# Mixers of a trunk layer traced as many small streams in the order of an in-order model of four engines

## The chip, the cores and the metric

The kernel runs on one core of a Trainium2 chip. Its five engines are TensorE (PE in the rows; PEld is its loading of weights), VectorE (DVE), ScalarE (ACT), GpSimd (POOL) and SyncE (SP), each with an instruction stream of its own that it works off in order; semaphores tie them together, and DMA queues move data between HBM and SBUF. The metric is the device time of one execution in microseconds (us).

## The reference

One layer of a decoder trunk on a sequence of 1024 tokens and a model width of 1024, in float32: half a SwiGLU feed-forward (2816 wide), then two token mixers side by side on the normed stream, then another half feed-forward. The mixers:

```python
proj = h @ w_in[l]
(c_q, k_a, v_a, k_idx, w_idx, q_b, k_b, v_b, gate_a, gate_b) = jnp.split(proj, offsets, axis=-1)
...
# a: sparse attention
dots = jnp.einsum('bthd,bsd->bths', qi, k_idx)
score = jnp.einsum('bths,bth->bts', jax.nn.relu(dots), wi)     # lightning indexer, 8 heads of 64
_, idx = lax.top_k(score, 256)                                 # the keys that a query may see
p = softmax(q_a . gathered keys)                               # 8 heads, one shared key and value
# b: stick-breaking attention, 8 heads of 64
log_not = jnp.where(strict, jax.nn.log_sigmoid(-z), 0.0)
between = lax.cumsum(log_not, axis=3, reverse=True) - log_not
a = jnp.where(strict, jnp.exp(jax.nn.log_sigmoid(z) + between), 0.0)
o = jnp.einsum('bhts,bshd->bthd', a, v_b)
...
merged = jax.nn.sigmoid(gate_a) * (y_a @ w_o_a[l]) + jax.nn.sigmoid(gate_b) * (y_b @ w_o_b[l])
x = x + merged @ w_out[l]
```

## The kernel before

Every product of two float32 matrices is made of three TensorE products of a high and a low part (`mm3`: high by high, low by high, high by low), so each operand is split: ScalarE copies the rounded high part, VectorE (or, for weights in SBUF, GpSimd) subtracts it and leaves the low part. The two feed-forward blocks and the merge stand before and after the mixers and are not touched here.

The mixers run in three stages, told apart below by what TensorE writes to PSUM.

- **Index stage.** `latents`, `keys`, `index_queries`, `indexer` and `queries` make the rotated keys and queries of the sparse attention (`psvb`, `pska`, `pskt`, `psq`, `psqt`) and the indexer's scores (`psdot`, ScalarE's `relu`, VectorE's `u`). Beside them `fillers` multiplies h by the value weights (`psvb`) and by the weights of q_b, k_b and the gates (`psf`); the results go to HBM through a ring of three 128x512 buffers, tag `ev`: `evv` for values, `evh` and `evl` (high, low) for q and k, `evg` for gates. Each filler's weights are loaded by SP (`wqk...r`), split into `...h` on ScalarE (L226) and `...l` on GpSimd (L228). `topk` finds the 256th largest score of each query by bisection, 3 row blocks at once, counting on ScalarE (`junka`, L1005) or VectorE (`junkv`, L1014), and stores a mask `bd`.
- **Stick stage.** `sticks` makes `psz` for 8 heads and 8 row blocks; ScalarE takes both sigmoids (L1334 `left`, L1335 `sa`), VectorE a scan along the keys (L1337) and a product (L1339, `sa`). `values` turns four blocks of `sa` at a time on TensorE (`pstT`), ScalarE and VectorE split them into `pt` (L1377, L1378), and TensorE multiplies by the values into one bank `psy` (L1362, L1364). The product of key block j is traced one step behind the turn of block j+1. The rest of `fillers` runs between.
- **Sparse stage.** `logits` (`psL`), softmax on ScalarE and VectorE (`e`), `latent_values` (`pspT`, `pt`, `pso`), `head_values` (`psya`, then `yah`, `yal`), and the two output projections `psob` and `psoa` (`project`), gated on GpSimd. The first `psm` ends it.

What sets the order: the stages are Python generators. `Weave.run` resumes again and again the generator whose wants are ready earliest by a model of the engines (`COST`: a fixed time and a rate for each). Only TensorE is under `manual_schedule` (L853): its instructions stand in the order in which they were traced, and those of the other engines are ordered by the framework's scheduler. In the model those engines fill earlier gaps (`place`, L111). A generator's evacuations are traced together with the matmuls that they follow. The sparse queries (`queries`, L1292) come after all index queries (the mark `wqi`). The heads of the stick stage take turns in two sets of buffers (`qs`, `kkh`, `kkl`, L1081).

## Time and profile before

| | us |
|---|---|
| median of 3 runs (lowest, highest) | 2362.55 (2357.9, 2365.03) |
| the profiled execution's own time | 2361.66 |
| its span in the trace | 2359.9 |
| TensorE busy in the span | 2221.0 |
| VectorE busy | 1628.2 |
| ScalarE busy | 1067.6 |
| GpSimd busy | 924.7 |
| index, stick and sparse stage | 715.8 to 987.3, 1365.5 and 1576.2 |

The mean granted TensorE clock over the span is 0.978 of full speed. Of the 2.3 us between the span and the execution's own time nothing is in the trace. A group in the rows below is a line, an engine and an operation; "idle before" is time in which that engine stood still right before instructions of the group, put down to what released it last.

### The profile page before, as it was taken

Reading aid. Unit: us, or ns where it says so; the run is one execution under the profiler, and the core shown is the slowest. Engines: PE = TensorE matmul, PEld = TensorE weight load, DVE = VectorE, ACT = ScalarE, POOL = GpSimd, SP = SyncE. Lnnn points to the kernel's source line nnn. Section 1 sums busy time; section 2 is a strip of 40 time slices with the busy share of each in tenths; the row PEclk is TensorE's granted clock in tenths of the full one; section 3 lists DMA queues with packets and bytes.
Section 4 is the critical chain, followed back from the end, with each engine's and each line's share of the span. In section 5 each row is a group of like instructions: output and inputs, shape, how many; then the busy total and the mean of one; then the engine's idle time right before and its main releaser. Section 6 shows DMA issues by size and latency. Waiting matters only on the chain.

```text
span 2359.9 us, 30282 instructions
## 1 busy us (share of the span) xinstructions
PE 2221.0 (94%) x10460; PEld 1819.9 (77%) x10460; DVE 1628.2 (69%) x2598; ACT 1067.6 (45%) x2042; POOL 924.7 (39%) x673
## 2 busy tenths in 40 slices
PE   7999999999998799778888989999999999999999
PEld 6788888888888678667666778777878888888877
DVE  5766666688772778699587877773476656667675
ACT  4323323344352378766745665643333333333443
POOL 3554555332352334311222223357435555552233
PEclk9999999999999999899899999999999999999999
DMA  5232333586753444434445532537423333348755
GB/s 162 84 108 94 107 94 107 182 318 218 191 162 112 110 110 121 134 74 95 103 120 130 170 107 101 185 126 259 125 65 97 107 94 108 98 156 283 235 174 179
DMA packets 251498, 330.65 MB, mean 140 GB/s; under 512 B 19536, under 2 KB 154336, under 8 KB 251344
## 3 DMA queue, kind: packets, MB, share of 16 engines
q1 hardware_dynamic: 234224, 288.83, 40.5%
q0 software_dynamic: 7488, 24.16, 2.8%
q10 hardware_dynamic: 9632, 15.73, 1.9%
q8 instruction: 82, 1.34, 0.2%
q14 instruction: 72, 0.59, 0.1%
HBM read 234.78 MB, written 93.88 MB: 139 GB/s over the span
## 4 chain that ended last, share of the span: by engine, by line
PE 40%; DVE 12%; issue 3%; DMA 2%; ACT 2%; POOL 1%; SPq 0%; ACTq 0%; DVEq 0%; POOLq 0%
PE p L609 3%; PE p L608 3%; PE p L607 3%; DVE left L1337 3%; PE pc L398 2%; PE pc L400 2%; PE pc L399 2%; PE pa L400 2%; PE pa L399 2%; PE pd L400 2%; PE pa L398 2%; PE pd L398 2%; PE pd L399 2%; DVE sa L1339 1%; DVE junkv L1014 1%
## 5 line engine op out<-in xcount | busy, mean ns | idle before, releaser
L1005 ACT ACTIVATE junka<-u,cand 128x640 bf16<-128x640 f32 (+1 forms) x138 | 124.9, 905 | 36.8 <-DVE cand L1003 29.4
L1337 DVE TENSOR_TENSOR_SCAN left<-left 128x640 f32<-128x640 f32 (+3 forms) x64 | 94.8, 1487 | 3.5 <-ACT left L1334 3.3
L1364 PE MATMUL psy<-pt,vv 128*128 128x512 f32 (+1 forms) x96 | 37.8, 405 | 36.5 <-DVE pt L1378 29.3
L1378 DVE TENSOR_TENSOR pt<-pstT,pt 128x512 fp32r<-128x512 f32 (+1 forms) x96 | 51.0, 550 | 26.8 <-ACT pt L1377 26.8
L1390 POOL TENSOR_TENSOR yl<-yt,yh 64x512 fp32r<-64x512 f32 x16 | 26.9, 1679 | 104.7 <-ACT yh L1389 94.0
L1510 DVE TENSOR_TENSOR pt<-pspT,pt 128x512 fp32r<-128x512 f32 x72 | 48.9, 686 | 26.8 <-ACT pt L1509 26.7
L1334 ACT ACTIVATE left<-psz 128x512 f32<-128x512 f32 (+2 forms) x96 | 48.6, 506 | 35.5 <-DVE sa L1339 20.9
L1470 ACT ACTIVATE e<-e,nm 128x768 f32<-128x768 f32 (+7 forms) x64 | 49.4, 772 | 32.2 <-DVE nm L1466 31.2
L217 POOL TENSOR_TENSOR rs<-ms,mhalf 128x1 f32<-128x1 f32 (+1 forms) x41 | 35.9, 909 | 68.9 <-DVE ms L215 67.9
L1377 ACT ACTIVATE pt<-pstT 128x512 fp32r<-128x512 f32 (+1 forms) x96 | 45.2, 495 | 38.0 <-PE pstT L1373 36.4
L1461 DVE CUSTOM_DVE_ANT_0 e<-psL,bias 128x512 f32<-128x512 f32 (+3 forms) x96 | 52.0, 550 | 9.4 <-PE psL L1459 8.6
L1286 DVE SCALAR_TENSOR_TENSOR u<-relu,WI,u 128x512 f32<-128x512 f32 (+1 forms) x70 | 49.3, 723 | 12.1 <-ACT relu L1281 10.3
L1339 DVE TENSOR_TENSOR sa<-sa,left 128x639 f32<-128x639 f32 (+3 forms) x64 | 53.6, 843 | 2.7
L1364 PEld LDWEIGHTS psy<-pt,vv 128*128 128x128 f32 x96 | 19.5, 203 | 46.3 <-DVE pt L1378 37.2
L608 PE MATMUL p<-bT,bS 128*128 128x512 f32 x132 | 51.8, 393 | 2.5 <-DVE bT L309 2.5
L1509 ACT ACTIVATE pt<-pspT 128x512 fp32r<-128x512 f32 x72 | 41.4, 594 | 27.7 <-PE pspT L1504 27.3
L609 PE MATMUL p<-bT,bS 128*128 128x512 f32 x132 | 51.6, 394 | 0.8 <-POOL bS L309 0.8
L608 PE MATMUL p<-aT,aS 128*128 128x512 f32 x132 | 51.7, 392 | 0.0
L609 PE MATMUL p<-aT,aS 128*128 128x512 f32 x132 | 50.9, 393 | 0.0
L1373 PE MATMUL pstT<-ident,sa 128*128 128x128 f32 x288 | 49.1, 292 | 1.3 <-DVE sa L1339 1.3
L1335 ACT ACTIVATE sa<-psz 128x512 f32<-128x512 f32 (+2 forms) x96 | 48.8, 509 | 0.0
L1281 ACT ACTIVATE relu<-psdot 128x512 f32<-128x512 f32 (+1 forms) x80 | 39.7, 521 | 19.9 <-DVE u L1286 10.2
(3061 smaller groups left out, 8423.1 us busy)
## 6 DMA issues: line engine op xcount, KB each, us to landing
aw<-in_w_down_dram SPq DMA_DIRECT2D x33, 512.0 KB, 4.5
bw<-in_w_down_dram SPq DMA_DIRECT2D x33, 512.0 KB, 4.5
a0r<-in_w_gate_dram SPq DMA_DIRECT2D x22, 512.0 KB, 4.1
a1r<-in_w_up_dram SPq DMA_DIRECT2D x22, 512.0 KB, 4.7
b0r<-in_w_gate_dram SPq DMA_DIRECT2D x22, 512.0 KB, 3.9
b1r<-in_w_up_dram SPq DMA_DIRECT2D x22, 512.0 KB, 4.8
x<-in_x_dram SPq DMA_DIRECT2D x16, 512.0 KB, 6.0
gd<-evg ACTq DMA_DIRECT2D x32, 256.0 KB, 2.3
```

Source lines behind the costliest of these rows:

```text
L398: nc.tensor.matmul(ps, a[:, c], b[k][:, HI], start=start and k == 0, stop=False, skip_group_check=True)
L399: nc.tensor.matmul(ps, a[:, c], b[k][:, LO], start=False, stop=False, skip_group_check=True)
L400: nc.tensor.matmul(ps, a[:, l], b[k][:, HI], start=False, stop=k == 3, skip_group_check=True)
L607: nc.tensor.matmul(ps[q][m], S[:, h], T[:, HI], start=p == 0, stop=False)
L608: nc.tensor.matmul(ps[q][m], S[:, h], T[:, LO], start=False, stop=False)
L609: nc.tensor.matmul(ps[q][m], S[:, l], T[:, HI], start=False, stop=p == last)
L1005: nc.scalar.activation(junks[1][:, 0:(i + 1) * P], score[i], AF.Sign, bias=cand.bitcast(F32)[:, b:b + 1], accum_out=cnt[:, b:b + 1])
L1337: nc.vector.tensor_tensor_scan(back, back, back, 1.0, op0=ALU.mult, op1=ALU.bypass)
L1339: nc.vector.tensor_mul(a[:, 0:nk - 1], a[:, 0:nk - 1], left[:, 1:nk])
L1364: nc.tensor.matmul(yp[:, off:512], vv[:, kc], pt[:, 512 + off:1024], start=False, stop=(j == 4 * c + 3), skip_group_check=True)
L1378: nc.vector.tensor_sub(pt[:, 512 + off:1024], tp[:, off:512], f32(pt[:, off:512]))
L1461: nc.vector.tensor_tensor_reduce(e[:, c], lp[:, 0:n_], bias[:, c], 1.0, LOW, op0=ALU.add, op1=ALU.max, accum_out=mx[:, g:g + 1])
```

## The change

The instructions of the mixers stay the same in kind, and nearly in number; the feed-forwards and the merge are not changed. What changes is how their order is made, and some buffers.

- **Order.** `manual_schedule` now holds TensorE, VectorE, ScalarE and GpSimd, so all four run the instructions of the mixers in the order of tracing. Each evacuation is a stream of its own (`spawn`); it names the engine of its next step and what that needs. `run` takes the stream with the least (time at which its step can start, rank, ready time plus slack). The model's engines work strictly in order, other `COST`s are put in, and a DMA's landing is modelled (2.4 us and 0.25 MB per us). SP is not held.
- **Rings.** Every buffer ring counts who still holds a tile (`give`). The stick stage's result takes one `ev` buffer (`yh`) in place of three; `yl` and `yt` share a ring of one. The gates of the output projections have a ring of three 512-column tiles in place of one of 1024.
- **Weights.** `Feed` keeps three sets of weights under way, through all fillers and both output projections.
- **Products.** The turns of `sa` and of `e` and the products with values are separate streams, so a product can stand any number of turns behind, with the ring `pt` three deep as before.
- **Sparse queries.** `queries` starts when the indexer's keys are done (`places`), with the buffers of the odd heads as its own; heads 1 to 7 wait for its end. The second half of the latents is turned first.

The core of the diff:

```diff
+    def __call__(self, name, holds=1):
+        w = self.weave
+        w.flush()
+        old = self.live[-self.bufs] if len(self.live) >= self.bufs else None
+        assert old is None or not w.held[old.tensor.name], name
+        t = self.tiles(name, self.tag, self.bufs, self.dt, self.shape)
+        if old is not None:
+            w.base[t.tensor.name] = max(w.base[t.tensor.name], w.done[old.tensor.name] + w.HOP)
+        w.held[t.tensor.name] = holds
+        self.live = (self.live + [t])[-self.bufs:]
+        return t
...
-    COST = {"PE": (0.0, 2400.0), "DVE": (0.07, 960.0), "Activation": (0.1, 1200.0), "Pool": (0.15, 460.0)}
+    COST = {PE: (0.015, 2400.0), DVE: (0.12, 960.0), ACT: (0.1, 1250.0), POOL: (0.2, 465.0)}
...
+                if eng == SP:
+                    self.free[SP] = max(self.free[SP], t) + mb / 0.25
+                    t, eng = self.free[SP] + 3.0, "DMA"
+                else:
+                    t = max(t, self.free[eng]) + (0.55 if eng == POOL else 0.05)
+                    self.free[eng], t, eng = t, t + 2.4 + mb / 0.25, "DMA"
...
+                eng, *needs = s.need
+                ready = max(self.when(needs, eng), s.since)
+                if ready < float("inf"):
+                    rank = next((n for n in needs if isinstance(n, int)), s.rank if eng == PE else min(s.rank, 1))
+                    slack = next((n for n in needs if isinstance(n, float)), 0.0)
+                    key = max(ready, self.free[eng] if eng != SP else 0.0), rank, ready + slack
+                    if best is None or key < best[0]:
+                        best = key, s
+            assert best, [(s.gen.__name__, s.need) for s in self.streams]
+            best[1].since = best[0][0]
+            self.step(best[1])
...
-    with fp as fpool, fps as fpsum, psm as psum, tc.manual_schedule(engines={nc.tensor.engine}):
-
-
-        ended = [0.0]
+    with fp as fpool, fps as fpsum, psm as psum, tc.manual_schedule(
+            engines={nc.tensor.engine, nc.vector.engine, nc.scalar.engine, nc.gpsimd.engine}):
...
+                while self.todo and len(self.coming) < 3:
...
+        sets[4:4] = [(w_in, C_VB + 256, 256, 4 * j, 4, f"wvb1{j}") for j in range(2)]
...
+        def qk_out(ps, pr, nh_, nl_, sc, cols):
+            yield ACT, ps, (evr, 2)
+            th, tl_ = evr("evh"), evr("evl")
+            nc.scalar.activation(th, ps, AF.Copy, scale=sc)
+            put_high(qkd[nh_][pr * P:(pr + 1) * P, cols], f32(th))
+            yield DVE, ps, th
+            nc.vector.scalar_tensor_tensor(tl_, ps, sc, f32(th), op0=ALU.mult, op1=ALU.subtract)
+            give(ps, th)
+            yield POOL, tl_
+            put_low(qkd[nl_][pr * P:(pr + 1) * P, cols], f32(tl_))
+            give(tl_)
...
+                yield SP, f"qk{h // 2}", "queries" if h else None, *rings
...
+            rows = [sring(f"cqn{half}") for half in range(2)]
             for half in (1, 0):
                 nc.sync.dma_start(rows[half], cqd[half])
-            yield None
-            weave.mark("wcq")
-            for half, cqn in enumerate(rows):
+                nc.sync.dma_start(*((rope, roped), (ropeq, ropeqd))[1 - half])
+            for half in (1, 0):
+                cqn, outs = rows[half], []
                 cols = slice(half * 512, half * 512 + 512)
...
+            yield PE, "places"
+
+            spare = [here[nm][1] for nm in ("qs", "kkh", "kkl")]
+            outs = []
             for t in range(NT):
-                QS = yield from qstack(W["uq"], t, qcos, qsin, True, "qsa")
-                put_low(qad[t * P:(t + 1) * P, :], f32(QS))
-
-        weave.run([latents(), keys(), indexer(), index_queries(), queries()], more)
+                QS = yield from qstack(WQ["uq"], t, qcos, qsin, True, "qsa", spare[t % 2], qxring, spare[2])
...
+        def turned_out(tp, pt, off=0):
+            yield ACT, tp
+            nc.scalar.activation(pt[:, off:512], tp[:, off:512], AF.Copy)
+            yield DVE, tp, pt
+            nc.vector.tensor_sub(pt[:, 512 + off:1024], tp[:, off:512], f32(pt[:, off:512]))
+            give(tp)
...
+        def y_out(yp, h, c):
+            yield ACT, yp, yring
+            yl = yring("yl")
+            yt = f32(yl[0:HD])
+            nc.scalar.activation(yt, yp[HD:P, :], AF.Copy)
+            yield DVE, yp, yl
+            nc.vector.tensor_add(yt, yp[0:HD, :], yt)
+            give(yp)
+            yield ACT, yl, evr
+            yh = evr("yh")
+            nc.scalar.activation(yh[0:HD], yt, AF.Copy)
+            cols = slice(c * 512, c * 512 + 512)
+            put_high(ybd[0][h * HD:(h + 1) * HD, cols], f32(yh[0:HD]))
+            yield POOL, yl, yh
+            nc.gpsimd.tensor_tensor(yl[0:HD], yt, f32(yh[0:HD]), op=ALU.subtract)
+            put_low(ybd[1][h * HD:(h + 1) * HD, cols], yt)
+            give(yl, yh)
...
+        def value_products(h, c, pts, outs):
+            yield PE, wbank, f"vv{h}"
+            yp, vv = wbank("psy"), VV[h]
+            for j in range(4 * c + 4):
+                while len(pts) <= j:
+                    yield PE, f"pt{h}{c}{j}"
+                job, off, pt = pts[j]
+                yield PE, job, pt
+
+                kc = slice(j * P, (j + 1) * P)
+                nc.tensor.matmul(yp[:, off:512], vv[:, kc], pt[:, off:512], start=(j == 0), stop=False,
+                                 skip_group_check=True)
+                nc.tensor.matmul(yp[:, off:512], vv[:, kc], pt[:, 512 + off:1024], start=False,
+                                 stop=(j == 4 * c + 3), skip_group_check=True)
+                give(pt)
...
-                yt = f32(evr("yt"))[0:HD]
-                nc.scalar.activation(yt, yp[HD:P, :], AF.Copy)
-                nc.vector.tensor_add(yt, yp[0:HD, :], yt)
-                yh, yl = (evr(n_)[0:HD] for n_ in ("yh", "yl"))
...
+        for g, rank in ((v_loads(), 0), (values(), 0), (sticks(), 1), (head_values(), 2), (latent_values(), 3), (logits(), 4),
+                        (hidden_keys(), 1), (latent_queries(), 1), (outputs(), 6)):
```

Three places in the order of instructions.

ScalarE at the start of the mixers, before the change: `wka0h` and `wka1h` are the high parts of the latent weights, `evv` the values' high parts, `cqh` the turned query latents.

```order
L226 ACTIVATE wka0h<-wka0r 128x1056
L902 ACTIVATE evv<-psvb 128x4x64 x3
L226 ACTIVATE wka1h<-wka1r 128x1056
L1127 ACT_TABLE_LOAD
L902 ACTIVATE evv<-psvb 128x4x64
L1164 ACTIVATE KK<-pska 128x128
L1166 ACTIVATE va<-pska 128x128
L1147 ACTIVATE cqh_6025<-pscqt,gcolq 128x512
```

And after it:

```order
L972 ACTIVATE evv<-psvb 128x4x64 x5
L1257 ACTIVATE cqh_6006<-pscqt,gcolq 128x512
L1257 ACTIVATE cqh_6007<-pscqt,gcolq 128x512
L972 ACTIVATE evv<-psvb 128x4x64
L1257 ACTIVATE cqh_6006<-pscqt,gcolq 128x512
L1257 ACTIVATE cqh_6007<-pscqt,gcolq 128x512
L938 ACTIVATE wka0h<-wka0r 128x1056
L972 ACTIVATE evv<-psvb 128x4x64
```

The split of the first latent weights stood ahead of the first four `evv`; now it stands behind five or more of them and the latents, and the split of the second is further down than these rows go.

TensorE at the second turn of keys, before the change: `kdup` is the duplicated key tile that VectorE makes, `pskt` its turn, `psf` the first filler with query weights.

```order
L239 MATMUL psvb<-wvb01h,mhi_5236 128x256
L240 MATMUL psvb<-wvb01l,mhi_5236 128x256
L241 MATMUL psvb<-wvb01h,mlo_5244 128x256
L1200 MATMUL pskt<-ident,kdup 128x128 x8
L239 MATMUL psf<-mhi_5229,wqk5200h 128x512
L240 MATMUL psf<-mlo_5237,wqk5200h 128x512
L241 MATMUL psf<-mhi_5229,wqk5200l 128x512
L239 MATMUL psf<-mhi_5230,wqk5200h 128x512
L240 MATMUL psf<-mlo_5238,wqk5200h 128x512
L241 MATMUL psf<-mhi_5230,wqk5200l 128x512
L1245 MATMUL psqt<-ident,qx 128x128 x4
```

And after it:

```order
L280 MATMUL psq<-wqih,cqh_6006 128x512
L281 MATMUL psq<-wqil,cqh_6006 128x512
L282 MATMUL psq<-wqih,cql_6008 128x512
L280 MATMUL psq<-wqih,cqh_6007 128x512
L281 MATMUL psq<-wqil,cqh_6007 128x512
L282 MATMUL psq<-wqih,cql_6009 128x512
L1485 MATMUL psdot<-kih,qsi 128x512
L1486 MATMUL psdot<-kil,qsi 128x512
L1372 MATMUL pskt<-ident,kdup 128x128 x4
L1485 MATMUL psdot<-kih,qsi 128x512
L1486 MATMUL psdot<-kil,qsi 128x512
L1485 MATMUL psdot<-kih,qsi 128x512
```

The second `pskt` stood behind value products; now it stands in the middle of the indexer's first `psdot`, split in two, behind the fillers of three sets of query and key weights.

TensorE at the end of the mixers, before the change: `psya` is the product with the value up-projection, `psm` the first matmul of the merge, `psoa` the output projection of the sparse attention.

```order
L241 MATMUL psya<-oh_14161,uvl 128x256
L239 MATMUL psya<-oh_14161,uvh 128x256
L240 MATMUL psya<-ol_14162,uvh 128x256
L241 MATMUL psya<-oh_14161,uvl 128x256
L239 MATMUL psya<-oh_14161,uvh 128x256
L240 MATMUL psya<-ol_14162,uvh 128x256
L241 MATMUL psya<-oh_14161,uvl 128x256
L239 MATMUL psm<-yah_11587,woa0h 128x512
L240 MATMUL psm<-yal_11591,woa0h 128x512
```

And after it:

```order
L282 MATMUL psoa<-yah_11598,oa6l 128x512
L280 MATMUL psoa<-yah_11599,oa6h 128x512
L281 MATMUL psoa<-yal_11603,oa6h 128x512
L282 MATMUL psoa<-yah_11599,oa6l 128x512
L280 MATMUL psoa<-yah_11600,oa6h 128x512
L281 MATMUL psoa<-yal_11604,oa6h 128x512
L282 MATMUL psoa<-yah_11600,oa6l 128x512
L280 MATMUL psm<-yah_11597,woa0h 128x512
L281 MATMUL psm<-yal_11601,woa0h 128x512
```

The products of the last head values ran straight into the merge; now matmuls of `psoa` stand between.

## Rows read from the trace of the kernel before

**Rows 1.** Busy time of each engine in four stretches: the indexer (first psvb to first psz), the sticks (to the last psy), the sparse attention (to the first psm), and a stretch of the first FFN. Columns: stretch, its length, busy us and instructions of PE, PEld, DVE, ACT, POOL, mean granted TensorE clock, share and rate of the DMA engines.

```profile
715.80:987.30 271.50, 231.69 (x1292) 200.64 (x1292) 176.79 (x335) 158.57 (x330) 102.57 (x95) 0.94 0.41 117
987.30:1365.50 378.20, 323.93 (x1531) 254.49 (x1530) 316.61 (x590) 242.56 (x515) 79.07 (x53) 0.93 0.45 116
1365.50:1576.20 210.70, 199.62 (x1058) 166.60 (x1057) 157.49 (x453) 122.24 (x255) 79.80 (x69) 0.97 0.43 141
177.00:590.00 413.00, 413.00 (x1795) 336.31 (x1794) 281.68 (x351) 143.88 (x250) 179.82 (x121) 1.00 0.48 160
```

**Rows 2.** Waits of TensorE from 700 to 990 us: engine, what it was to write, its line, what it waited for; us in total, times, the longest.

```profile
PE psqt L1245 <- DVE qx L1241: 10.9, 3, 10.2
PE psdot L1278 <- ACT relu L1281: 9.2, 8, 3.4
PE pskt L1200 <- DVE kdup L1192: 9.1, 2, 8.7
PE psf L239 <- DVE evl L934: 4.9, 2, 3.4
PE psvb L239 <- DVE evv L903: 3.4, 1, 3.4
PE psvb L239 <- DVE cqn L669: 2.6, 1, 2.6
PE pska L240 <- POOL wka1l L228: 2.1, 1, 2.1
```

**Rows 3.** The same view from 990 to 1366 us.

```profile
PE psy L1364 <- DVE pt L1378: 29.3, 22, 4.4
PE psy L1362 <- ACT pt L1377: 8.1, 7, 2.4
PE psy L1364 <- DVE rem L1070: 7.0, 1, 7.0
PE psf L239 <- ACT evg L952: 5.9, 3, 5.4
```

**Rows 4.** Timeline of ScalarE from 714 us, where the latent weights are split: start, length, what; in brackets the idle time before it.

```profile
723.32 1.08 ACT L226 ACTIVATE wka0h<-wka0r 128x1056 fp32r<-128x1056 f32 x1 [9.52 <-issue]
724.31 0.64 ACT L902 ACTIVATE evv<-psvb 128x256 fp32r<-128x256 f32 x2
```

**Rows 5.** Timeline of VectorE around the second set of keys.

```profile
771.55 2.79 DVE L1182 TENSOR_TENSOR KK<-KK,rs 128x512 f32<-128x512 f32 x1
774.38 5.19 DVE L1183 TENSOR_TENSOR KK<-KK,gk 128x512 f32<-128x512 f32 x1
779.60 0.69 DVE L1187 TENSOR_TENSOR kt<-KK,rope 128x512 f32<-128x512 f32 x1
```

**Rows 6.** Timeline of GpSimd in the same stretch.

```profile
771.39 2.40 POOL L228 TENSOR_TENSOR wuql<-wuqr,wuqh 128x1024 fp32r<-128x1024 f32 x1
...
774.36 2.36 POOL L228 TENSOR_TENSOR wqk5200l<-wqk5200r,wqk5200h 128x1024 fp32r<-128x1024 f32 x1
776.66 2.35 POOL L228 TENSOR_TENSOR wqk10320l<-wqk10320r,wqk10320h 128x1024 fp32r<-128x1024 f32 x1
```

**Rows 7.** Groups of VectorE instructions in the sticks' stretch: line, what, count, busy us and mean ns of one, idle time before them and its releasers.

```profile
L1337 DVE TENSOR_TENSOR_SCAN left<-left 128x640 f32<-128x640 f32 (+3 forms) x64 | 94.8, 1487 | 3.5 <-ACT left L1334 3.3
L1339 DVE TENSOR_TENSOR sa<-sa,left 128x639 f32<-128x639 f32 (+3 forms) x64 | 53.6, 843 | 2.7
L1378 DVE TENSOR_TENSOR pt<-pstT,pt 128x512 fp32r<-128x512 f32 (+1 forms) x96 | 51.0, 550 | 26.8 <-ACT pt L1377 26.8
L1014 DVE TENSOR_SCALAR_CACHE_REDUCE junkv<-word,clow 128x1024 bf16<-128x1024 uint16 (+2 forms) x48 | 41.9, 873 | 0.7
```

**Rows 8.** Groups of GpSimd instructions in the same stretch; the sixteen splits of weights (L228) stand one by one, one of them shown.

```profile
L1390 POOL TENSOR_TENSOR yl<-yt,yh 64x512 fp32r<-64x512 f32 x15 | 25.6, 1706 | 98.3 <-ACT yh L1389 87.6 <-DMA gd<-evg 10.7
...
L228 POOL TENSOR_TENSOR wg11l<-wg11r,wg11h 128x1024 fp32r<-128x1024 f32 x1 | 2.4, 2362 | 16.5 <-ACT wg11h L226 16.5
```

**Rows 9.** DMA issues from 800 to 990 us: queue, count, KB each, median us from issue to landing.

```profile
qhd<-evh ACTq DMA_DIRECT2D x8, 256.0 KB, 5.5
qld<-evl POOLq DMA_DIRECT2D x8, 256.0 KB, 7.6
khd<-evh ACTq DMA_DIRECT2D x8, 256.0 KB, 3.1
kld<-evl POOLq DMA_DIRECT2D x8, 256.0 KB, 5.2
```

**Rows 10.** Timeline of TensorE at the end of the mixers.

```profile
1564.49 0.65 PE L1496 MATMUL pso<-pt,kkh 128*128 128x512 f32 x1 [2.89 <-ACT e L1470]
...
1567.45 0.47 PE L1504 MATMUL pspT<-ident,e 128*128 128x128 f32 x1 [0.82 <-DVE e L1473]
1568.67 0.79 PE L1496 MATMUL pso<-pt,kkh 128*128 128x512 f32 x1 [0.75 <-ACT pt L1509]
...
1576.18 0.50 PE L239 MATMUL psm<-yah,woa0h 128*128 128x512 f32 x1 [0.93 <-DVE yal L1544]
```

1033 lines of the change are left out of this document (616 added, 417 removed).

## The prediction

> **What bounds the kernel now.** I read the page's busy shares first, then busy time by stage, then TensorE's waits, then what the engines that it waits for did just before. Over the stretch of FFN in [rows 1] TensorE is busy for all of 413.0 us at full clock, 0.230 us for each of 1795 matmuls: nothing that the mixers do can shorten that. In the mixers it is busy 231.7 of 271.5, 323.9 of 378.2 and 199.6 of 210.7 us, so it stands still for 39.8, 54.3 and 11.1 us, together 105 us. Beside that the mean granted clock there is 0.94, 0.93 and 0.97. With busy time times the missing share as the price (an estimate) the lower level, 1.2 in place of 2.4 GHz, costs 13.9, 22.7 and 6.0 us. It falls after TensorE has stood still or waited in short pieces; the FFN stretch, with no gap, keeps 1.00. So some 148 us is the most that any order of the same instructions can win on TensorE, and the next limit must be looked for: in the stick stage VectorE is busy 316.6 us [rows 1], most of it scans, products and low parts [rows 7]. That stage cannot fall below some 317 us without VectorE falling too. In the other two stages VectorE has some 95 and 53 us to spare.
>
> Which wait ends last is read from [rows 2, 3]. In the index stage there are two long single ones, 10.2 us for `qx` and 8.7 us for `kdup`, and a crowd of short ones for `relu`. In the stick stage the products wait 29.3 + 8.1 us for `pt`, in 29 pieces, then once 7.0 us for `rem` and 5.9 us for gates.
>
> **The change part by part.** It neither adds nor removes work: each engine keeps nearly the same instructions. So each term is a wait that goes, stays or appears.
>
> Front of the index stage. ScalarE stood still 9.52 us with the split of `wka0h` at the head of its stream and the values' high parts behind it [rows 4]; the row names no releaser, and I take it to be the raw weights' landing. TensorE paid 3.4 us for `evv`, and 2.1 us for `wka1l` later [rows 2]. The split now stands behind the first `evv`. If the weights are late again, TensorE has values to multiply. I take 3.4 + 2.1 = 5.5 us as gone; the 2.6 us for `cqn` ends ahead of the stretch in [rows 1] and stays.
>
> Second keys. The 8.7 us for `kdup` come from VectorE: two products on 512 columns took 2.79 and 5.19 us [rows 5], where a like one took 0.69 us right after. In those 8 us GpSimd ran weight splits of 2.40, 2.36 and 2.35 us [rows 6], and the 5.19 us product ends just as the last two do. So these two products lost 6.6 us to GpSimd. The order now puts the turn behind fillers and the first `psdot`, some 38 matmuls of 0.230 us or 8.7 us more cover than before. The whole wait of 9.1 us goes, even if GpSimd holds the products as long again. Also, `qx` is behind these products on VectorE: its 10.2 us is the same jam seen from the next stream. I take 10 us of 10.9 as gone.
>
> What appears: the first query weights need buffers that come free when the value products are done, so the fillers that now give cover begin with a split on ScalarE and one of 2.36 us on GpSimd. I charge 4 us (bounds: 0, if the weights wait for nothing, and 10, the longest wait in [rows 2]).
>
> The `relu` waits (9.2 us) stay: the scores still have two such buffers. So does the 4.9 us for `evl`: queries and keys still leave through a ring of three.
>
> The clock: with the long waits gone I give back half of 13.9 us, 7 us; bounds 0 and 14.
>
> Index stage: 5.5 + 9.1 + 10 + 7 - 4 = 27.6 us less.
>
> Stick stage. The 5.9 us for `evg` has its cause in the `ev` ring: the results of a head took three of its buffers, and GpSimd waited 87.6 us for `yh` in them [rows 8]. With one buffer in place of three this goes. The 7.0 us for `rem` is a step of the mask that VectorE ran in one piece ahead of `pt`; the change yields between its steps, so it goes: 12.9 us. Of 37.4 us for `pt` I take a third, 12.5 us. Products may stand further behind turns now, but `pt` must still pass ScalarE and then VectorE, which is busy 84% of the stage, and the scans before it are the same (1487 ns on average, 64 of them, up to the next free place [rows 7]). Bounds are 0 and all 37.4. Of the clock I take a third, 8 us (0 to 23). Sum 33.4 us: the stage comes to 345 us, 28 above VectorE's busy time.
>
> Sparse stage. At its end TensorE waits 2.89, 0.82, 0.75 and 0.93 us within some 14 us and runs slowly between [rows 10]. Matmuls of `psoa` now stand behind the last attention work. They fill such gaps but came from elsewhere, where they filled others: 2 us (bounds -3 to 17, the stage's idle and clock).
>
> Sum: 27.6 + 33.4 + 2 = 63 us. The profiled execution took 2361.66, so 2298.7, say **2299 us**. That execution is 0.9 us below the median of the three runs, so I make no correction. It is 2.7% faster. What this kernel's measurement can tell from no change is about 0.3%, or 7 us.
>
> **The rule that speaks against it.** The jam in [rows 5, 6] says that a VectorE product with two inputs in SBUF stands still while GpSimd runs a product of its own.
>
> The Trainium skill, GPSIMD Engine Reference, section Key points, says the same: GpSimd shares its SBUF interfaces with VectorE, with contention against VectorE instructions in a 2-port mode or with two SBUF inputs. The trace agrees (5.19 beside 0.69 us). The model that makes the new order counts each engine alone, so by this rule its plan breaks wherever it sets a split beside a product; that is the slower rival below.
>
> **The rivals.**
>
> *Landings eat the index gain.* The new order counts on a transfer of 256 KB landing some 3.5 us after its issue; measured are 5.5 and 7.6 us for the halves of the queries, 3.1 and 5.2 us for those of the keys [rows 9]. Each of 16 halves takes two of three `ev` buffers, and they come free only upon landing. TensorE makes a half in 24 x 0.230 = 5.5 us. A landing of 7.6 us holds the next but one half by about 2 us, if no other stream fills it: 16 x 2 = 32 us. Then 2299 + 32 = 2331. For it: `psf` waited for `evl` before, and fillers now begin earlier and stand closer. Against: that wait was only 4.9 us.
>
> *Everything goes.* All idle of the index stage (39.8) and 5 us of its clock, the stick stage down to VectorE's 316.6 (61.6 less), 5 us in the sparse stage: 111 us, 2250. For it: streams are now cut small enough for any gap to be filled. Against: the plan's durations are not the chip's, and engines that work in order hand each error on.
>
> *Slower: GpSimd holds VectorE in the stick stage.* All evacuations are in order now, and nothing steps ahead of a held one. GpSimd is busy 79.1 us there [rows 1], with 15 subtractions of 1706 ns and 16 splits of 2362 ns or more [rows 8], all with two inputs. VectorE has the `sa` product, 64 times 843 ns, just in the chain scan, `sa`, turn, `pt` [rows 7]. If all 79 us came to hold that chain, TensorE would wait as much for `pt`: 2299 + 79 = 2378, slower by 0.7%. It decides from 63 us, four fifths of GpSimd's time. For it: one jam cost 6.6 us within 8. Against: before the change some of it was paid already, and scans have one input.
>
> *No change.* Each wait that goes comes back under another name, the work in front of `pt` above all, since VectorE is the busiest after TensorE: 2362 us.
>
> **How the numbers follow.** The forecast gets 0.46, landings 0.18, everything 0.12, no change 0.09, slower 0.15. Faster by over 0.3%: 0.46 + 0.18 + 0.12 = 0.76; within 0.3%: 0.09; slower: 0.15. The forecast's own range is 2275 to 2325, from half of the bounds above. The wide one takes in landings and no change, and leaves out the outer half of "everything" and the upper half of "slower": 2258 to 2366.
>
> **What would show it.** In the changed profile: no wait over 5 us for `qx` or `kdup` in the index stage, which ends some 244 us after its start; no `rem` or `evg` wait, and some 25 us for `pt`, in a stick stage of 345 us with VectorE's busy time at 305 to 320 us; a granted clock of 0.96 or more in both. Landings would show as `psf` waiting for `evl` or the DMA queues of `evh` over 20 us; contention as a mean `sa` well over 843 ns. The forecast is wrong if TensorE's idle time in the mixers falls by less than 30 or more than 80 us of its 105.

## The result and the profile after

The changed kernel takes 2347.57 us (median of 8 runs, 2343.23 to 2349.67), the kernel before 2358.61 us on the same chips (8 runs, 2353.92 to 2365.03): ratio 0.9947, 95% interval 0.9930 to 0.9964. That is faster by 0.5%, and far from the 2299 us that was forecast. Of 63 us foreseen, some 12 came (11.0 by the medians, 12.5 by the ratio).

The two profiled executions took 2361.66 and 2345.06 us, so the traces lie 5.6 us further apart than the medians. Their spans are 2359.9 and 2343.0 us, so 1.8 and 2.1 us lie outside the traces (for the kernel before it is 1.8 us and not 2.3). Busy time by stage in the changed kernel, in the columns of [rows 1]; the last row is all that follows the mixers:

```profile
715.40:974.00 258.60, 234.27 (x1299) 198.41 (x1300) 169.49 (x330) 150.89 (x311) 101.52 (x95) 0.97 0.42 120
974.00:1327.40 353.40, 308.45 (x1505) 245.20 (x1503) 325.67 (x569) 244.18 (x522) 92.80 (x54) 0.94 0.48 125
1327.40:1555.40 228.00, 203.39 (x1076) 169.20 (x1075) 159.46 (x490) 128.07 (x268) 74.37 (x67) 0.94 0.37 121
1555.40:2343.00 787.60, 775.34 (x3404) 630.38 (x3404) 487.48 (x585) 272.93 (x461) 354.37 (x232) 0.99 0.46 152
```

Against [rows 1] the index stage is 12.9 us shorter, the stick stage 24.8, and the sparse stage 17.3 us longer. What follows the mixers took 783.7 us before and takes 787.6. TensorE's idle time (length less busy time) went from 39.8, 54.3 and 11.1 us to 24.3, 45.0 and 24.6. Together that is 11.3 us less of 105, where the prediction called itself wrong below 30. The row of the kernel before for what follows the mixers:

```profile
1576.20:2359.90 783.70, 771.33 (x3404) 627.80 (x3404) 488.16 (x585) 272.79 (x461) 349.48 (x226) 1.00 0.45 150
```

TensorE's waits in the index stage, to be read against [rows 2]:

```profile
PE psdot L1485 <- ACT relu L1455: 8.1, 11, 1.7
PE psqt L1428 <- DVE qx L1424: 7.1, 5, 3.2
PE pskt L1372 <- DVE kdup L1361: 4.1, 1, 4.1
...
PE psf L282 <- POOL wqk5200l L940: 1.6, 1, 1.6
PE psvb L280 <- DVE evv L974: 1.4, 1, 1.4
PE psf L280 <- DVE evl L1019: 1.0, 1, 1.0
```

In the stick stage, against [rows 3]:

```profile
PE pstT L1649 <- DVE sa L1552: 28.9, 10, 5.5
PE pstT L1649 <- DVE pt L1598: 12.9, 14, 2.8
PE psy L1631 <- DVE pt L1598: 2.0, 3, 1.4
```

The waits of `psy` for `pt`, 37.4 us in [rows 3], are all but gone, and those for gates and `rem` with them. In their place TensorE waits 41.8 us (1.3 before the change) one step earlier in the same chain, before the turn `pstT`: for `sa`, and for a PSUM bank whose last reader is VectorE. The row of the kernel before for that turn:

```profile
PE pstT L1373 <- DVE sa L1339: 1.3, 1, 1.3
```

In the sparse stage:

```profile
PE psm L280 <- ACT o L1850: 9.2, 1, 9.2
PE psL L1737 <- DVE mx L1699: 5.9, 4, 4.0
PE psoa L280 <- ACT o L1850: 4.0, 2, 3.2
PE pso L1772 <- ACT pt L1596: 3.5, 1, 3.5
```

The first and third are new and stand at the end. The second was 0.4 us before and stands at the start, where a bank for logits waits for VectorE's maxima `mx`. ScalarE and GpSimd at the end, by their timelines:

```profile
1546.82 0.60 ACT L1850 ACTIVATE o<-psoa 128x512 f32<-128x512 f32 x1
1554.71 0.60 ACT L1850 ACTIVATE o<-psoa 128x512 f32<-128x512 f32 x1 [7.30 <-DMA md<-o]
```

```profile
1546.99 2.34 POOL L269 TENSOR_TENSOR woa2l<-woa2r,woa2h 128x1024 fp32r<-128x1024 f32 x1 [2.05 <-ACT woa2h L267]
1549.28 1.26 POOL L1858 TENSOR_TENSOR o<-o,other 128x512 f32<-128x512 f32 x1
1550.84 0.58 POOL L1859 DMA_DIRECT2D md<-o  x1 [0.30 <-POOL o L1858]
1551.44 1.27 POOL L1855 TENSOR_TENSOR o<-o,gate 128x512 f32<-128x512 f32 x1
1552.80 1.26 POOL L1858 TENSOR_TENSOR o<-o,other 128x512 f32<-128x512 f32 x1
```

The last result of the output projection can't leave its bank: ScalarE's copy `o` needs a buffer of the ring `ev`, and the buffer holds an earlier result until its store `md` has landed, issued at 1550.84. GpSimd issues that store behind a product, a sum and a weight split of the merge. So the merge's first matmul is 9.2 us late, and those behind it follow at the lower level of the clock, 0.43 us from start to start where 0.23 is usual.

VectorE's two dearest groups in the stick stage, against [rows 7]: the scan is as before, the product of scan and sigmoid takes 994 in place of 843 ns.

```profile
L1549 DVE TENSOR_TENSOR_SCAN left<-left 128x640 f32<-128x640 f32 (+3 forms) x64 | 94.4, 1477 | 1.4 <-ACT left L1541 1.2
L1552 DVE TENSOR_TENSOR sa<-sa,left 128x639 f32<-128x639 f32 (+3 forms) x64 | 63.5, 994 | 3.4
```

### The profile page after: what moved, and what is told of

Read it like the earlier page. It is cut to its first block, busy times and chain, and to the rows that moved or that the text cites. A ratio compares the mean times of both kernels' runs of the same rounds, so it can differ in the third digit from the quotient of the medians.

```text
span 2343.0 us, 30206 instructions
## 1 busy us (share of the span) xinstructions
PE 2216.0 (95%) x10460; PEld 1813.7 (77%) x10460; DVE 1629.6 (70%) x2596; ACT 1067.8 (46%) x2042; POOL 935.9 (40%) x675
## 4 chain that ended last, share of the span: by engine, by line
PE 69%; DVE 16%; issue 5%; DMA 4%; ACT 4%; POOL 2%; SPq 0%; ACTq 0%; DVEq 0%; POOLq 0%
PE p L649 6%; PE p L650 6%; PE p L648 6%; PE pc L439 3%; PE pc L441 3%; PE pc L440 3%; PE pd L441 3%; PE pd L439 3%; PE pd L440 3%; PE pa L441 3%; PE pa L439 3%; PE pa L440 3%; DVE left L1549 2%; PE pb L439 2%; PE pb L441 2%
## 5 line engine op out<-in xcount | busy, mean ns | idle before, releaser
L1615 POOL TENSOR_TENSOR yl<-yl,yh 64x512 fp32r<-64x512 f32 x16 | 32.3, 2022 | 149.1 <-ACT yh L1611 149.1
L1649 PE MATMUL pstT<-ident,sa 128*128 128x128 f32 x288 | 52.0, 295 | 41.9 <-DVE sa L1552 28.9
L1649 PEld LDWEIGHTS pstT<-ident,sa 128*128 128x128 f32 x288 | 37.2, 150 | 57.1 <-DVE sa L1552 31.2
L1855 POOL TENSOR_TENSOR o<-o,gate 128x512 f32<-128x512 f32 x24 | 30.8, 1285 | 112.1 <-ACT o L1850 109.9
L1552 DVE TENSOR_TENSOR sa<-sa,left 128x639 f32<-128x639 f32 (+3 forms) x64 | 63.5, 994 | 3.4
L1711 ACT ACTIVATE e<-e,nm 128x768 f32<-128x768 f32 (+7 forms) x64 | 49.4, 774 | 21.2 <-DVE nm L1706 20.6
L1598 DVE TENSOR_TENSOR pt<-pstT,pt 128x512 fp32r<-128x512 f32 (+1 forms) x96 | 50.6, 548 | 10.5 <-ACT pt L1596 10.1
L649 PE MATMUL p<-bT,bS 128*128 128x512 f32 x132 | 52.7, 399 | 2.7 <-DVE bT L350 2.7
L650 PE MATMUL p<-bT,bS 128*128 128x512 f32 x132 | 52.4, 399 | 0.8 <-POOL bS L350 0.8
L648 PE MATMUL p<-bT,bS 128*128 128x512 f32 x132 | 46.4, 392 | 0.0
```

The lines of the kernel that those rows point to most:

```text
L648: nc.tensor.matmul(ps[q][m], S[:, h], T[:, HI], start=p == 0, stop=False)
L649: nc.tensor.matmul(ps[q][m], S[:, h], T[:, LO], start=False, stop=False)
L650: nc.tensor.matmul(ps[q][m], S[:, l], T[:, HI], start=False, stop=p == last)
L1552: nc.vector.tensor_mul(a[:, 0:nk - 1], a[:, 0:nk - 1], left[:, 1:nk])
L1598: nc.vector.tensor_sub(pt[:, 512 + off:1024], tp[:, off:512], f32(pt[:, off:512]))
L1649: nc.tensor.transpose(tp[:, q * P:(q + 1) * P], A[n + q][:, j * P:(j + 1) * P], ident)
```

## The experiments

Unless said otherwise an edit is made to the changed kernel. Each run was timed against the kernel before on the same chip. Ratios are to the kernel before; the changed kernel's own is 0.9947.

### The end of the sparse stage: e1, e5, e2, e11

**e1.** Six buffers for the last projection's results.

```diff
-            yield ACT, ps, evr
-            o = f32(evr("o"))
+            ring = pring if row < ND and row % 2 else evr
+            yield ACT, ps, ring
+            o = f32(ring("o"))[:, 0:512]
```

> The changed kernel, with every second result of the last output projection (psoa) copied into a buffer of the ring pt, which is idle by then, in place of the ring ev: six buffers in place of three at the end of the sparse stage. Theory A (the end of the sparse stage waits for buffers: a copy o waits until the store md of the copy three before it has landed, and the bank that psm needs waits for that copy): TensorE's 0.8, 3.2 and 9.2 us before psoa, psoa and psm go, and so do some 4 us of low clock behind them; about 17 us less than the changed kernel, 2330 us, ratio to the kernel before 0.988. Rival B (GpSimd's gating and its stores are late anyway, and whatever comes next waits for them): the wait moves to the merge, and the time stays within 5 us of the changed kernel, ratio 0.993 to 0.997.

2341.72 us, ratio 0.9931 (0.9911 to 0.9951). The sparse stage falls from 228.0 to 214.9 us, but what follows takes 796.5 in place of 787.6. TensorE's waits from the last turns to the end:

```profile
PE psout L280 <- ACT m L349: 10.1, 1, 10.1
...
PE psm L280 <- ACT o L1851: 1.5, 1, 1.5
```

The wait moved into the merge, as B had it: more buffers let GpSimd fall further behind, and the merge waits for it 32 us later.

**e5.** e1, and the gating of that projection on VectorE.

```diff
-            yield POOL, o, gate
-            nc.gpsimd.tensor_tensor(o, o, gate, op=ALU.mult)
-            for t in other:
-                yield POOL, o, t
-                nc.gpsimd.tensor_tensor(o, o, t, op=ALU.add)
+            eng, unit = (DVE, nc.vector) if row < ND else (POOL, nc.gpsimd)
+            yield eng, o, gate
+            unit.tensor_tensor(o, o, gate, op=ALU.mult)
+            for t in other:
+                yield eng, o, t
+                unit.tensor_tensor(o, o, t, op=ALU.add)
+                yield POOL, o
```

> The kernel of e1 (six buffers for the results of the last projection), with the gating of that projection, a product and a sum per result, on VectorE in place of GpSimd. Theory A (after e1, GpSimd's row of two products, a store and a weight split for each of eight results, some 4.4 us each where TensorE makes one in 2.8, is what the merge waits 10.1 us for at psout): VectorE, idle there, does each pair in some 1.4 us, the wait goes with its low clock, 10 to 12 us less than e1: 2330 us, ratio 0.988. Rival B (the gates' loads, of which three buffers allow one and a half results at a time, are late by themselves): psout or psoa still waits over 5 us, ratio 0.991 to 0.995.

2337.7 us, ratio 0.9921 (0.9900 to 0.9941). Sparse stage and what follows, where e1 had 214.9 and 796.5 us:

```profile
1328.80:1543.60 214.80, 201.68 (x1078) 168.67 (x1076) 166.52 (x501) 128.20 (x268) 55.56 (x51) 0.96 0.36 118
1543.60:2334.00 790.40, 774.11 (x3404) 628.54 (x3404) 492.99 (x591) 272.85 (x461) 354.13 (x231) 1.00 0.47 154
```

The 10.1 us at `psout` are gone, as A had it; the traces of e1 and e5 differ by 6.6 us, the intervals overlap. With both edits the two stretches together are 10.4 us shorter than in the changed kernel (1005.2 against 1015.6), and still 10.8 us longer than in the kernel before (994.4). In e5 TensorE waits 6.0 us for `mx` at the start of the stage (0.4 before the change), and 6.0 us in four pieces for GpSimd's weight splits in the merge (2.4 us before the change). So e5 gives back about half of what these stretches lost.

**e2.** The projections chosen ahead of turns and logits: `(outputs(), 6)` becomes `(outputs(), 2)`.

> The changed kernel with the output projections given rank 2 in place of 6, so that they are chosen ahead of turns and logits of the sparse attention when both could start. Theory A (the projections were put off to the end, where TensorE has nothing else and meets the gating chain): they run beside the attention again, the wait of 9.2 us before psm goes; but the attention's own last chain then stands at the end, as in the kernel before, and costs some 8 us with low clock. Net 8 to 12 us less than the changed kernel, 2337 us, ratio 0.991. Rival B (the sparse stage's loss is not where the projections stand but in-order engines): no change, ratio 0.993 to 0.997.

2363.42 us, ratio 1.0023 (1.0013 to 1.0034): neither theory. The projections are used up at the start of the sparse stage, where VectorE falls idle in turn, as its 7.92 us of 30 in the second row shows:

```profile
1329.50:1579.70 250.20, 219.62 (x1078) 173.67 (x1076) 158.93 (x490) 128.59 (x268) 80.27 (x72) 0.93 0.37 120
1360.00:1390.00 30.00, 30.00 (x143) 24.84 (x142) 7.92 (x27) 11.78 (x21) 16.41 (x16) 1.00 0.38 127
```

Afterwards the attention has nothing to cover its chain: TensorE waits 9.3 us for `pt` on ScalarE, in 11 pieces, where it waited 3.5. The projections are the cover of this stage, and of the two ranks tried the later one is better.

**e11.** e5, with the first projection's loads allowed earlier: `yield SP, "uv"` becomes `yield SP, "c"`.

> The kernel of e5, with the loads for the first output projection allowed as soon as the stick stage's buffers are free, ahead of the loads and the split of the value up-projection. Theory A (at the start of the sparse stage TensorE waits some 10 us for logits and turned weights because no projection can run there yet): those waits fall to 4 us or less and the low clock with them, 6 to 9 us less than e5: 2330 us, ratio 0.989. Rival B (the loads take as long as the waits last, or push others back): within 3 us of e5, ratio 0.991 to 0.994.

2341.49 us, ratio 0.9933 (0.9918 to 0.9948): no gain, B. At the start `pso` waits 2.0 in place of 3.6 us, but `psL` 7.1 in place of 6.0, and 5.4 us come up at `psya`, for VectorE; the sparse stage takes 222.0 us, 7 more than in e5.

### What holds the stick stage: e3, e4, e6, e8

**e3.** The lower 16 bits of the first group's thresholds counted on ScalarE: `if gi:` ahead of the second `by_sign` becomes `if True:`.

> The changed kernel, with the lower 16 bits of the first three row blocks' thresholds counted on ScalarE, as for the other three, in place of VectorE (48 counts of 873 ns and the small steps with them leave VectorE, 48 of some 905 ns come to ScalarE). Theory A (the stick stage is at VectorE's limit: busy 325.7 of 353.4 us): VectorE falls by some 45 us there and the stage by 20 to 30 us, to TensorE's 308 us and its waits; 2320 us, ratio 0.984. Rival B (the chain from scan over product and turn to pt sets the stage, not the sum of VectorE's work): the stage stays within 7 us, and ScalarE's longer share may add; ratio 0.992 to 0.998.

2357.48 us, ratio 0.9993 (0.9983 to 1.0003). Two stretches, first of the changed kernel, then of e3:

```profile
1000.00:1120.00 120.00, 98.64 (x460) 77.79 (x461) 115.67 (x250) 83.25 (x179) 23.23 (x13) 0.90 0.40 90
1240.00:1327.00 87.00, 75.14 (x383) 59.60 (x384) 78.19 (x101) 51.24 (x110) 22.58 (x15) 0.92 0.51 160
```

```profile
1000.00:1120.00 120.00, 114.24 (x567) 92.03 (x566) 74.46 (x137) 107.16 (x238) 28.86 (x15) 0.99 0.48 109
1240.00:1337.00 97.00, 55.20 (x256) 41.05 (x256) 87.02 (x135) 51.51 (x113) 20.25 (x14) 0.77 0.36 107
```

By the time it is neither, just past B's 0.998; by the stretches each theory holds in its place. While thresholds are counted, VectorE is the limit: 115.67 of 120 us busy, and with the counts gone TensorE rises from 98.64 to 114.24. But what TensorE does earlier is the fillers, and they are missing at the end: there it is busy 55.20 of 97 us with VectorE at 87.02, and not one `psf` falls into that stretch, where the changed kernel has 129. The last mask is stored at 1328.2 in place of 1290.3 us. That this lateness is what heaps VectorE's work up at the end was not tried by itself.

**e4.** TensorE alone held to the traced order:

```diff
-            engines={nc.tensor.engine, nc.vector.engine, nc.scalar.engine, nc.gpsimd.engine}):
+            engines={nc.tensor.engine}):
```

> The changed kernel with TensorE alone held to the traced order, as before the change; VectorE, ScalarE and GpSimd are ordered by the framework's scheduler again, all buffers and the order on TensorE as in the changed kernel. Theory A (what was won comes from TensorE's order and the buffers, and holding the others adds little): 2340 to 2352 us, ratio 0.992 to 0.997. Rival B (TensorE's new order needs the others in the modelled order): waits for pt, sa and kdup grow and the time is 2365 us or more, ratio 1.003 or more. Rival C (the hold itself costs, since nothing overtakes a late operation): 2335 us or less, ratio 0.990 or less.

2362.36 us, ratio 1.0012 (0.9998 to 1.0025), between A's 0.997 and B's 1.003, so neither. The three stages:

```profile
714.30:965.70 251.40, 229.22 (x1298) 196.98 (x1299) 163.00 (x323) 141.19 (x295) 99.29 (x95) 0.98 0.41 118
965.70:1337.10 371.40, 316.57 (x1504) 250.53 (x1503) 315.72 (x566) 250.51 (x538) 81.77 (x55) 0.93 0.47 122
1337.10:1572.10 235.00, 207.28 (x1077) 168.03 (x1075) 155.42 (x490) 127.07 (x268) 75.67 (x68) 0.96 0.37 120
```

The order on TensorE, the buffers and the streams are the same: without the traced order on the other three engines (the hold in these expectations) nothing is won. That order costs 7 us in the index stage and gives 18 and 7 us in the other two.

**e6.** The traced order on all four engines from the stick stage on: `manual_schedule` with TensorE alone is left behind the run of the index stage, and entered again with all four.

> The changed kernel, with VectorE, ScalarE and GpSimd held to the traced order from the stick stage on alone; in the index stage the framework's scheduler orders them, as in e4. Theory A (the hold costs in the index stage, where e4 took 251 us and the changed kernel 259, and pays in the stick and sparse stages, where e4 took 25 us more): index stage 251, the rest as in the changed kernel, 2340 us, ratio 0.991. Rival B (what the index stage wins comes back in the stick stage, whose first heads find later masks or queries): ratio 0.993 to 0.997.

2344.90 us, ratio 0.9949 (0.9933 to 0.9964): B. The first `psz` comes 46 us earlier than in the changed kernel, with 150 more matmuls left for the stretch behind it, and the stick stage ends at 1327.6 us, where the changed kernel's ends at 1327.4: over the two stages nothing is won.

**e8.** The sparse queries put back behind the index queries: `yield PE, "places"` becomes `yield PE, "places", "wqi"`.

> The changed kernel with the sparse queries put back behind the last index queries. Theory A (their place beside the indexer fills TensorE there, and heads of the stick stage wait for their end): the index stage or the first heads lose 6 to 12 us, 2356 us, ratio 0.999. Rival B (the place of the queries matters little, since fillers can take their place): within 4 us of the changed kernel, ratio 0.993 to 0.997.

2353.31 us, ratio 0.9985 (0.9975 to 0.9995), so their new place is worth about 9 us (0.9985 less 0.9947, of 2358): A by the time. That the wait for their end is what costs it was not tried apart.

### VectorE beside GpSimd, and the plan that doesn't know of it: e7, e9, e10, e13, e14, e16

The timelines of the changed kernel show once more that GpSimd holds VectorE up (the hold, from here on). A product of 1023 columns on VectorE takes 1.23 us at 1001.28, and 3.26 us at 1103.41, beside a split on GpSimd that begins just before it:

```profile
1001.28 1.23 DVE L1552 TENSOR_TENSOR sa<-sa,left 128x1023 f32<-128x1023 f32 x1
...
1103.41 3.26 DVE L1552 TENSOR_TENSOR sa<-sa,left 128x1023 f32<-128x1023 f32 x1
```

```profile
1103.25 2.33 POOL L940 TENSOR_TENSOR wg15l<-wg15r,wg15h 128x1024 fp32r<-128x1024 f32 x1 [3.49 <-ACT wg15h L938]
```

**e7.** GpSimd's sixteen subtractions for the gates' weights become copies from one input, so the gates' weights have no low part of their own.

```diff
-                nc.gpsimd.tensor_tensor(wl[:, 0:m], raw[:, 0:m], f32(wh[:, 0:m]), op=ALU.subtract)
+                (nc.gpsimd.tensor_copy(wl[:, 0:m], raw[:, 0:m]) if nm.startswith("wg") else
+                 nc.gpsimd.tensor_tensor(wl[:, 0:m], raw[:, 0:m], f32(wh[:, 0:m]), op=ALU.subtract))
```

> The changed kernel, with GpSimd's sixteen subtractions that split the gates' weights replaced by copies of the same size from one input; the low part of these weights is then the whole weight, so the gates are not the reference's. Theory A (GpSimd's two-input work holds VectorE in the stick stage: the product of scan and sigmoid takes 994 ns on average there, 843 before the change): its mean falls below 900, TensorE's wait for sa falls from 28.9 to under 22 us, and the time by 5 to 10 us: 2340 us, ratio 0.991. Rival B (those longer products are hidden, or come from the yl subtractions, which stay): within 3 us of the changed kernel, ratio 0.993 to 0.997.

2324.3 us, ratio 0.9866 (0.9845 to 0.9887): what A foresaw, and twice as much. The stick stage, and its product:

```profile
970.80:1306.80 336.00, 302.18 (x1504) 240.31 (x1503) 305.15 (x568) 244.92 (x524) 70.72 (x54) 0.97 0.51 132
```

```profile
L1553 DVE TENSOR_TENSOR sa<-sa,left 128x639 f32<-128x639 f32 (+3 forms) x64 | 53.7, 840 | 3.4
```

VectorE's busy time falls by 20.5 us with not one of its instructions changed, the wait for `sa` from 28.9 to 19.3 us, the stage by 17.4. But A's reason, the two inputs on GpSimd, does not hold up. Beside a copy the same product of 1023 columns, 1.23 us alone, took 1.80:

```profile
1141.93 1.55 POOL L940 CAST wg2l<-wg2r 128x1024 fp32r<-128x1024 f32 x1 [1.66 <-PE psf L282]
```

```profile
1142.75 1.80 DVE L1553 TENSOR_TENSOR sa<-sa,left 128x1023 f32<-128x1023 f32 x1
```

So copies from one input hold VectorE as well. They are shorter, most of them 1.04 to 1.1 us where the subtractions took 2.33 and more, and hold it for less time; whether the second input adds anything is not shown.

**e9.** The same edit in the kernel before.

> The kernel before the change, with its sixteen subtractions for the gates' weights on GpSimd replaced by copies from one input, as in e7; the gates are then not the reference's. Theory A (the change brought the hold: its order puts these subtractions beside products of VectorE, as the longer mean of 994 against 843 ns says): the kernel before gains little from it, 0 to 5 us, ratio 0.998 to 1.000. Rival B (the hold is paid in both kernels alike, and e7's 20 us are no explanation of what the change failed to bring): 12 us or more, ratio 0.995 or less.

2342.97 us, ratio 0.9935 (0.9920 to 0.9950): B. The stick stage, its scan and its product, against [rows 1, 7]:

```profile
985.90:1348.20 362.30, 319.39 (x1529) 250.34 (x1528) 303.96 (x590) 242.02 (x515) 59.35 (x53) 0.95 0.48 121
```

```profile
L1340 DVE TENSOR_TENSOR_SCAN left<-left 128x640 f32<-128x640 f32 (+3 forms) x64 | 86.7, 1360 | 3.5 <-ACT left L1337 3.3
L1342 DVE TENSOR_TENSOR sa<-sa,left 128x639 f32<-128x639 f32 (+3 forms) x64 | 53.9, 847 | 3.3
```

The stage goes from 378.2 to 362.3 us, VectorE's busy time there from 316.6 to 304.0. The product's mean hardly moves (843 to 847 ns), but the scan's falls from 1487 to 1360: before the change most of the hold lay on the scans (8.1 of 12.6 us), and a mean of 843 ns for the product did not show it. So the kernel before paid about 15 us for these subtractions, and the changed one pays about 19 (0.9947 less 0.9866). The change added some 4 us, no more than the intervals' width; the rest was there.

**e10.** The model of the engines counts two-input operations of VectorE and GpSimd as excluding each other.

```diff
-                t = max(t, self.free[eng]) + self.cost(i, eng, outs, ins)
+                two = eng in (DVE, POOL) and sum(a.space != PSUM and a.free_size() > 64 for a in ins) > 1
+                t = max(t, self.free[eng], self.port if two else 0.0) + self.cost(i, eng, outs, ins)
                 self.free[eng] = self.last = t
+                if two:
+                    self.port = t
```

> The changed kernel, whose model of the engines now lets an operation of VectorE with two inputs in SBUF and one of GpSimd exclude each other; nothing else is changed, the order follows. Theory A (the plan goes wrong because it counts these engines as independent): waits for sa shrink, the stick stage by 5 to 12 us; 2339 us, ratio 0.991. Rival B (knowing of the hold does not take it away, and nothing else is there to put in its place): within 4 us of the changed kernel, ratio 0.993 to 0.997. Rival C (a model that is stricter than the chip moves work behind others for nothing): 2352 us or more, ratio 0.9975 or more.

2330.56 us, ratio 0.9879 (0.9862 to 0.9895): what A foresaw, and more. Index and stick stage:

```profile
715.10:969.00 253.90, 240.17 (x1355) 207.86 (x1356) 169.36 (x322) 147.03 (x300) 104.78 (x96) 0.97 0.44 124
969.00:1313.30 344.30, 299.26 (x1447) 234.69 (x1446) 317.32 (x574) 248.81 (x533) 87.89 (x53) 0.93 0.49 127
```

In the index stage TensorE gets 56 more matmuls in and stands still 13.7 in place of 24.3 us; the sticks end 14 us earlier. The wait for `sa` falls from 28.9 to 21.5 us and the product's mean from 994 to 941 ns, 840 in e7: the hold has become less, and is not gone.

**e13.** Instead, the model takes VectorE's operations as 7% longer: `self.cost(...)` times 1.07 where the engine is VectorE.

> The changed kernel, whose model takes every operation of VectorE as 7% longer; no exclusion of GpSimd. Theory A (e10 gains because the plan knows where the two engines hold each other): a plan that is only slower on VectorE gains little, within 5 us of the changed kernel, ratio 0.992 to 0.997. Rival B (e10 gains because any order that allows VectorE more time is better): 2333 us or less, ratio 0.990 or less. Rival C (orders scatter by ten or more us whatever the model says): slower than the kernel before is possible, ratio 0.999 or more.

2353.88 us, ratio 0.9978 (0.9968 to 0.9988), slower than the changed kernel by some 7 us: B falls, and the ratio lies between A's and C's. Index and stick stage together take 610.4 us, where the changed kernel takes 612.0 and e10 598.2; the loss is in the sparse stage, 237.8 in place of 228.0 us. So a plan that is merely stricter gains little where e10 gains 14 us, and orders scatter by several us for no reason that was looked for. That e10 gains because it keeps the two engines apart is argued and not shown: VectorE's busy time over the two stages, 495.2 us in the changed kernel, is 486.7 in e10, and 487.2 in e13 as well.

**e14.** e10 and e7 together.

> e10, with GpSimd's sixteen subtractions for the gates' weights replaced by copies from one input as in e7 (the gates are not the reference's). Theory A (both gains are the hold, once avoided and once known): together less than their sum, 4 to 12 us less than e10; 2322 us, ratio 0.984. Rival B (they are different things): the sum, 17 + 20 us, 2310 us, ratio 0.979.

2321.04 us, ratio 0.9843 (0.9827 to 0.9860): A. The copies, worth 19 us without the exclusion, are worth about 8 with it (0.9879 less 0.9843, of 2358). So some 11 of the 16 us of e10 overlap with the copies' gain; that speaks for the hold, though two gains that run into a third limit would look alike.

**e16.** e10 with TensorE alone held, as in e4.

> The kernel of e10 with TensorE alone held to the traced order, as in e4. Theory A (the plan pays only where the engines that it plans follow it): the gain is lost as in e4, 2350 us or more, ratio 0.997 or more. Rival B (TensorE's better order is what counts): within 6 us of e10, ratio 0.986 to 0.991.

2385.52 us, ratio 1.0110 (1.0092 to 1.0127): A. The better plan is the slowest of all these kernels when three of its engines don't follow it; its stick stage takes 378.3 us.

### Repairs of two stages together: e12, e15

**e12** is e11 with e10's model.

> e11 with the model of e10. If both theories A hold, their gains add: 2322 us, ratio 0.985; if only that of e11, 2330 us, ratio 0.989; if neither, that of e5, 0.992.

2323.74 us, ratio 0.9851 (0.9836 to 0.9866). That is the number for both theories, but e11's had failed: the gains of e10 and e5 alone add to it (0.9879 plus 0.9921 less 0.9947 is 0.9853).

**e15** is e10 with the edits of e5.

> e10, with the copies and the gating at the end of the sparse stage as in e5. Theory A (the two repairs lie in different stages and add): 10 us less than e10, 2321 us, ratio 0.984. Rival B (the end of the mixers is set by something that neither touches): 2327 us or more, ratio 0.9865 or more.

2320.35 us, ratio 0.9836 (0.9820 to 0.9853): A. Its stick stage is as in e10, its sparse stage as in e5:

```profile
969.90:1314.10 344.20, 296.99 (x1447) 233.19 (x1446) 317.36 (x574) 248.74 (x533) 88.43 (x53) 0.94 0.49 127
1314.10:1528.60 214.50, 201.57 (x1078) 168.41 (x1076) 165.52 (x499) 127.84 (x268) 55.54 (x51) 0.96 0.36 118
```

It is 1.6% faster than the kernel before, three times what the change gave.

## Why the prediction was wrong

The direction was right, the size was not: 0.5% in place of 2.7%. By its own terms:

| term | foreseen, us | in the traces, us |
|---|---|---|
| front of the index stage | -5.5 | -4.1 (`evv` 3.4 to 1.4, `wka1l` gone) |
| second keys, `kdup` | -9.1 | -5.0 |
| `qx` | -10 | -3.8 |
| new wait for the first query weights | +4 | +1.6 |
| `relu` and `evl` | 0 | -5.0 |
| clock of the index stage | -7 | +2.6 in busy time, 1.6 of it (an estimate) for 7 more matmuls |
| gates and `rem` in the stick stage | -12.9 | -12.9 |
| `pt` in the stick stage | -12.5 | -35.4, and +40.5 at `pstT` |
| clock of the stick stage | -8 | -15.5 in busy time, 6 of it (an estimate) for 26 matmuls that moved |
| sparse stage | -2 | +17.3, and +3.9 behind it |

**The sparse stage** is the largest miss, 23 us with what follows, and beyond its bounds. The step that failed is "They fill such gaps but came from elsewhere". I counted the moved `psoa` as TensorE work and asked only what it covers. What each of them issues at its new place was not counted: a copy that needs a buffer, two loads, and on GpSimd a product, a sum and a store, beside the merge's weight splits. One after another, without attention work between, they meet GpSimd's limit. e1 and e5 show it: buffers move the wait, the other engine removes it, and e15 repeats the gain on e10's order. That is 10.4 of the 21.2 us lost here; the other half stands, in e5, in longer waits of `psL` at the start of the stage and for weight splits in the merge; no run shows its cause, and the one attempt on the start (e11) failed.

**The stick stage** was 8.6 us too optimistic. Of 37.4 us for `pt` I took a third as gone. Nearly all went, and more than that came back one step earlier. That is the fourth rival, "Each wait that goes comes back under another name, the work in front of `pt` above all", in one stage. The forecast saw VectorE as the next limit through its sum, with 28 us to spare; e3 shows it binding for the stretch in which thresholds are counted and not over the stage.

**The index stage** was 14.7 us too optimistic. I took two waits as gone whole that shrank by half, though the trace had shown the hold behind them (6.6 us of two products) and the order doesn't know of it. With the exclusion in the model `kdup` no longer appears among the waits (e10), but `qx` stays at 7.2 us, so the hold is not shown to be its cause. The clock term failed in its price: the granted clock rose from 0.94 to 0.97, as foreseen, and the busy time that was to fall by 7 us did not fall. So busy time times the missing share was no measure here of what a better clock gives back; no run says why.

**The slower rival** had its mechanism right and its price wrong. It named that some of the hold was paid before and gave that no number; e9 measures 15 us, e7 the whole as 19, so 4 are new. Its "scans have one input" was wrong as well: in the code the scan's two inputs are the same row, and in e9 its mean falls from 1487 to 1360 ns. Its sign, a mean of `sa` well over 843 ns, came, but that mean told where the hold lay and not how much of it there was. The sentence on the plan, that it "breaks wherever it sets a split beside a product", points at what the change left to win: with the exclusion in the model it is 16 us faster (e10), with VectorE slower in the model it is not (e13), with the reservations made there.

The Trainium skill, GPSIMD Engine Reference, section 1, Specifications, names the condition: contention on the shared SBUF interfaces with VectorE instructions in a 2-port mode or with two SBUF inputs. The trace agrees (3.26 beside 1.23 us for one product).

**Landings** played no part in the index stage, where `psf` waits 1.0 us for `evl`. That nothing is won without the traced order on all four engines (e4) I had not foreseen; I put the gain down to buffers and to TensorE's order. Whether that order alone, without the new buffers, would win anything was not tried.

Open is what ends the stick stage: in e6 its first `psz` comes 46 us earlier and its end at the same time, and no run isolates the cause.

## What to carry to other kernels

When work moves, price at its new place everything that it issues, on the engine that is slowest there, and look for a wait that goes one step earlier in the same chain. A static order for several engines depends on what its model knows of how they hold each other: here an exclusion that takes a few lines in the model gave more than the whole change, though how much of that is the hold avoided stays open; and a plan that some engines don't follow can be worse than none. A mean that looks normal can hide a hold that lies on another instruction, so take the whole engine's busy time with and without it. More buffers in front of a slow engine move a wait, and a faster engine ends it.
